# Weight loads on ScalarE's DMA queue, other transfers on the sync queue: a hybrid stick-breaking and retention step on one core

## The chip, the core and the metric

The kernel runs on one core of a Trainium2 chip. The metric is the device time of one execution in microseconds (us), as the median of several runs; lower is better. The core has five engines with a queue of instructions each: TensorE (PE, matrix products; its weight loads are listed as PEld), VectorE (DVE), ScalarE (ACT), GpSimd (POOL) and SyncE (SP). DMA transfers are issued by instructions that stand in the queue of SP, ACT or POOL; the profile writes such an entry as SPq or ACTq, and under POOL.

## The reference

One inference step of a one-layer encoder, all in float32. There are 1024 frames of a new prompt and 8 running streams of 16 frames (128 rows, "the sample"), each row 2048 wide.

```python
h = rms_norm(x, norm_pre)
q_sb, k_sb, v_sb, gate_sb, q_r, k_r, v_r, gate_r = split(h @ w_in)     # 8 x 1024 columns
q_r, k_r = rope(q_r, pos), rope(k_r, pos) * HEAD_DIM ** -0.5
# heads A (8 of 128): stick-breaking attention, strictly causal
a = exp(log_sigmoid(z) + reverse_cumsum_of(log_sigmoid(-z)));  o_sb = a @ v
# heads B (8 of 128): retention with a decay per head, in chunks of 64, with a running state S
o_r = (q k^T * decay) @ v + (q @ S) * decay_read;  S = S * g + k^T (v * decay_write)
y = concat(head_norm(o_sb) * silu(gate_sb), head_norm(o_r) * silu(gate_r)) @ w_out
x = x + rms_norm(y, norm_post)
```

The sample's attention also reads a cache of 1024 past keys and values per stream, its retention starts from a given state. Keys, values and states are outputs too.

## The kernel before

**Products.** Each float32 operand is split into a high part (ACT, a copy that rounds, line 166) and a low part (DVE, a subtraction, line 167), and each product is three matmuls: high by high, high by low, low by high. ACT and DVE therefore handle every block of weights before PE may use it. A raw block `wr` has five buffers, a split block `wh`/`wl` four.

**Stages.** The rows are worked in two groups. Group one (phase 0 in the code) holds row tiles 0 to 3 and the sample, 640 rows; group two (phase 1) holds tiles 4 to 7. Within a group the 8 heads follow each other. For a head, `rows_of_head` makes values and gates (`project_rows`, products at line 451, weights `wrn` loaded at line 442); `project` makes keys and queries of both kinds (products at line 394, weights `wr` loaded at line 383). Then follows the output product with `w_out` (lines 1195 to 1199, weights loaded at line 1212 by `load_split`), done with seven block products instead of eight, so that sums of operand blocks are made beforehand (`sums`, line 301) and left operands are loaded and split by `left` (lines 318 to 338).

**What runs beside the products.** Attention, retention, the head norms and the sums are generators ("jobs"). Each product calls `tick`, which advances a count and lets at most one due job do its next piece; the number that a job yields is the count of ticks until its next piece. The constants named `D_...` are these paces; of a pair, the first is for group one, the second for group two. From this the build fixes the order of the instructions in every engine's queue. A queue is then worked in that order, whatever is ready at run time.

**Rotary parts.** `rope` (line 491) reads a PSUM accumulator: ACT copies the swapped halves into `sw` (lines 495, 496), DVE multiplies `sw` by the sines (497), the accumulator by the cosines (498) and adds (499). The accumulator's bank is free for the next product when ACT's copies and the cosine product have read it. `sw` has one buffer.

**Turning tiles.** Several tiles are transposed by a way through DRAM: `turn_out` (line 634) writes the tile to a scratch tensor, `turn_in` (line 640) reads it back by four DMAs with exchanged block indices, and DVE transposes the 32x32 blocks. This is done for the retention keys (`s_rk`, lines 1016 to 1021), for each head's output (`s_o`, lines 703 to 717, in `Out.finish`), for the attention weights (`s_be`, by POOL) and for the sample's attention weights (`s_bd`).

**Row norms.** The root of each row's mean square is needed before values leave PSUM. `squares` (line 528) loads the rows and squares them on ACT: for group one during the first `rows_of_head`, for group two in a job started after it. `spread` (line 551) lays the roots out along a row by four matmuls (line 558).

**Queues.** SP issues the weight loads, the loads of rows, caches and operands and the read-backs `turn_in` of `s_rk`, `s_o` and `s_bd`. ACT issues the writes: `turn_out` of `s_rk`, `s_o`, `s_bd`, the stores of keys, values and states, of the sums, and the copy of the input rows into the output (`residuals`, line 367). POOL issues the loads of cached keys (line 802) and both ways of `s_be`.

Of the kernel before, what the change touches and what calls it, by code (L numbers as in the profile page):

```python
# [28 lines left out]
WQ = 4  # L29
D_X = (5, 4)  # L30
X_PIECES = ((0, 256), (256, 384), (640, 512))
# [15 lines left out]
D_TB = (17, 24)  # L47
D_TI = (36, 13)
D_OUT = 3
V_SET = 4  # L50
# [37 lines left out]
def tile_hybrid_step(  # L88
# [290 lines left out]
    def load_w(col):  # L379
        hs, ls = [], []  # L380
        for w in range(KT // WQ):
            wr = wp.tile([P, WQ, P], F32, name="wr", tag="wr", bufs=5)
            nc.sync.dma_start(wr, w_cols[COLS.index(col[0]), col[1], :, w * WQ : (w + 1) * WQ, :])
# [49 lines left out]
    def project_rows(g, mov, part, extra, out, loads=None, ready=None):  # L433
# [31 lines left out]
    with ExitStack() as s1:  # L465
# [25 lines left out]
        def rope(acc, tag, cosT, sinT):  # L491
            e = ep.tile([P, NMAX], F32, name=tag, tag=tag)
            for a, (o, m) in acc:
                sw = ep.tile([P, 512], F32, name="sw", tag="sw", bufs=1)
                nc.scalar.activation(sw[0:64, :m], a[64:128, :m], AF.Copy)
                nc.scalar.activation(sw[64:128, :m], a[0:64, :m], AF.Copy)
                nc.vector.tensor_tensor(sw[:, :m], sw[:, :m], sinT[:, o : o + m], ALU.mult)
                nc.vector.tensor_tensor(e[:, o : o + m], a[:, :m], cosT[:, o : o + m], ALU.mult)  # L498
                nc.vector.tensor_tensor(e[:, o : o + m], e[:, o : o + m], sw[:, :m], ALU.add)
            return e  # L500
# [11 lines left out]
        with tc.tile_pool(name="p0", bufs=2) as p0, tc.tile_pool(name="p0s", bufs=1) as p0s, tc.tile_pool(  # L512
# [48 lines left out]
            def second_panel(w):  # L561
                wr = wp.tile([P, WQ, P], F32, name="wr", tag="wr", bufs=5)
                nc.sync.dma_start(wr, w_cols[COLS.index(5), 0, :, w * WQ : (w + 1) * WQ, :])
# [51 lines left out]
            nc.scalar.dma_start(s_root, rb)  # L615

# [9 lines left out]
        def store_rows(tiles, n, dst_p, dst_s, h):  # L626
            nc.scalar.dma_start(dst_p[h, :, tiles[0] : tiles[0] + 4, :], n[:, :4, :])
            if SAMPLE in tiles:
                nc.scalar.dma_start(dst_s[h], n[:, 4, :])

        qp = kq.tile([P, 2, P], F32, name="qp")
        nc.vector.memset(qp, 0.0)

        def turn_out(src, tag, q=nc.scalar):

            s = scr.tile([src.shape[1], P, P], F32, name=tag)
            q.dma_start(s.rearrange("k q c -> q k c"), src)
            return s

        def turn_in(s, raw, q):  # L640
# [52 lines left out]
        class Out:  # L693
# [9 lines left out]
            def finish(self, b, gi, h, at, oT, dst):  # L703
# [12 lines left out]
                nc.vector.tensor_scalar(flat, oT[:, :n], gains[:, b, h : h + 1], None, ALU.mult)  # L716
                nc.scalar.dma_start(dst, flat)

# [176 lines left out]
        def retention(gi, g, h, out, rq, rk, rkn, rv, dT):  # L895
# [14 lines left out]
            for i in range(4):  # L910
# [31 lines left out]
                yield D_RET[phase[0]]  # L942
            nc.scalar.dma_start(s_S[h] if gi == 0 else s_prompt[0, 0, h], S)
            if SAMPLE in g["tiles"]:
                yield from sample_retention(h, out, sc, rq, rkn, rv)

        def sample_retention(h, out, sc, rq, rkn, rv):
# [57 lines left out]
            for c in range(4):  # L1005
                nc.scalar.dma_start(s_sample[h, :, 2 * c : 2 * c + 2, :], sts[c])

        def ret_branch(gi, g, h, rows_in, rk):
# [22 lines left out]
        def sb_branch(gi, g, h, out, q2, k2, kT, rest):  # L1031
            tiles, nt = g["tiles"], len(g["tiles"])
            off = 0 if gi == 0 else 4
            nc.scalar.dma_start(k_prompt[h, :, tiles[0] * P : (tiles[0] + 4) * P], kT[:, :NB_TOK])
            if SAMPLE in tiles:
                nc.scalar.dma_start(k_sample[h], kT[:, 4 * P : 5 * P])
            if gi == 0:
                nc.scalar.dma_start(s_k[h], kT[:, :NB_TOK])
            yield D_NAT[phase[0]]
            yield from stick_breaking(g, h, out, q2, k2, rest)  # L1040
            store_rows(tiles, values[gi, h][:, :, 0, :], v_prompt, v_sample, h)
            if gi == 0:
                nc.scalar.dma_start(s_v[h], values[gi, h][:, :4, 0, :])
            yield from out.finish(0, gi, h, 0, kT, s_y[gi][h][:, :NB_TOK])
# [238 lines left out]
    with ExitStack() as s3:  # L1283
# [78 lines left out]
        def all_of(made):  # L1362
# [60 lines left out]
        def keep_blocks():  # L1423
            for k in range(HT):
                wr = wp.tile([P, 512], F32, name="wr3", tag="wr", bufs=5)
                pin(nc.sync.dma_start(wr, weights_of(4, 1, k)))
                yield 1
# [143 lines left out]
```

## Time and profile before

| | us |
|---|---|
| median of 3 runs | 2281.82 (2278.89 to 2284.04) |
| the profiled execution's own time | 2282.22 |
| its span, first to last instruction | 2280.5 |
| PE busy in it | 2229.1 |
| DVE, ACT, POOL busy | 1272.2, 926.8, 343.7 |

The profile is one execution. Its page gives busy times, the chain of work that ended last and the costliest groups of instructions; the trace behind it answers narrower questions: who waited for whom, what ran in a given stretch, and when each DMA was issued. A row of the timeline has the start, the duration, engine, line, operation, the tiles written and read, the shape, a count where equal neighbours are merged, and in brackets the idle time of the engine before it with what ended it. A row of the waits has the waiting instruction, what it waited for, the total in us, the number of times and the longest. A row of the stretches has the stretch, its length, the busy time of PE, PEld, DVE, ACT and POOL (with counts), then the granted share of PE's clock, the DMA share and GB/s.

### The profile page before, as it was taken

The page shows a single profiled execution, that of the slowest core. Times are in us where ns is not written, and L with a number is a line of the kernel's source. Part 1 is how long each engine was busy: PE and PEld are TensorE (multiplying, and loading weights), DVE is VectorE, ACT ScalarE, POOL GpSimd, SP SyncE. Part 2 cuts the span into 40 slices and gives each one's busy share as a digit, 9 for nine tenths or more (in the row PEclk, how much of TensorE's full clock was granted, in tenths as well). Part 3 has the DMA queues.
Part 4 walks back from the last instruction along what each step waited for, and adds up shares of the span by engine and source line. Part 5 has one row for each costly group of instructions (what it writes and reads, how often), then busy time and mean ns, then how long its engine had stood idle before and what let it go on. Part 6 is the DMA issues. An engine that isn't in the chain of part 4 may idle for free.

```text
span 2280.5 us, 34787 instructions
## 1 busy us (share of the span) xinstructions
PE 2229.1 (98%) x12002; PEld 1891.4 (83%) x12002; DVE 1272.2 (56%) x2724; ACT 926.8 (41%) x1995; POOL 343.7 (15%) x577
## 2 busy tenths in 40 slices
PE   8999999999999999999999999999999999989998
PEld 7888889798888979797778888888888887768886
DVE  5345445453454445355556665656666657556667
ACT  6433333333333333334333343443433445545563
POOL 0011020212102020111202111120302113000020
PEclk9999999999999999999999999999999999999999
DMA  8566665576756657677768887888887777765785
GB/s 285 170 202 176 198 184 179 179 193 209 185 182 183 200 176 193 187 202 256 193 177 221 247 226 235 226 240 226 239 248 225 220 209 202 223 203 158 216 221 171
DMA packets 442354, 471.25 MB, mean 207 GB/s; under 512 B 182848, under 2 KB 298560, under 8 KB 441664
## 3 DMA queue, kind: packets, MB, share of 16 engines
q1 hardware_dynamic: 319936, 308.55, 46.7%
q0 software_dynamic: 28720, 78.41, 12.6%
q10 hardware_dynamic: 93520, 82.07, 11.4%
q8 instruction: 94, 1.54, 0.3%
q14 instruction: 84, 0.69, 0.1%
HBM read 367.97 MB, written 110.36 MB: 210 GB/s over the span
## 4 chain that ended last, share of the span: by engine, by line
PE 83%; DMA 6%; issue 4%; DVE 4%; ACT 2%; SPq 1%; ACTq 0%; DVEq 0%; POOL 0%; POOLq 0%
PE accm L451 34%; PE acc L394 27%; PE a L1195 4%; PE a L1199 4%; PE a L1198 4%; PE pa L777 2%; PE z L750 2%; PE zc L817 1%; PE pd L878 1%; DMA wr<-w_out 1%; DMA ro<-s_rk 1%; DMA mr<-s_s 1%; PE pa L917 1%; PE rs L899 1%; ACT wh L166 1%
## 5 line engine op out<-in xcount | busy, mean ns | idle before, releaser
L451 PE MATMUL accm<-whn,mh 128*128 128x512 f32 x1152 | 453.5, 394 | 4.0 <-DVE rq L498 3.9
L394 PE MATMUL acc<-mh,wh 128*128 128x256 f32 (+2 forms) x1536 | 445.0, 340 | 12.6 <-ACT wh L166 9.3
L451 PE MATMUL accm<-wln,mh 128*128 128x512 f32 x1152 | 452.5, 393 | 0.5 <-DVE wln L167 0.5
L451 PE MATMUL accm<-whn,ml 128*128 128x512 f32 x1152 | 452.9, 393 | 0.0
L394 PE MATMUL acc<-mh,wl 128*128 128x256 f32 (+2 forms) x1536 | 447.3, 342 | 0.3 <-DVE wl L167 0.3
L394 PE MATMUL acc<-ml,wh 128*128 128x256 f32 (+2 forms) x1536 | 446.4, 341 | 0.0
L166 ACT ACTIVATE wh<-wr 128x512 fp32r<-128x512 f32 x408 | 256.2, 631 | 466.3 <-PE acc L394 168.2
L167 DVE TENSOR_TENSOR wl<-wr,wh 128x512 fp32r<-128x512 f32 x408 | 278.8, 687 | 274.1 <-ACT wh L166 259.9
L167 DVE TENSOR_TENSOR wln<-wrn,whn 128x512 fp32r<-128x512 f32 x256 | 175.5, 689 | 290.4 <-ACT whn L166 279.2
L166 ACT ACTIVATE whn<-wrn 128x512 fp32r<-128x512 f32 x256 | 160.9, 632 | 413.3 <-PE accm L451 240.0
L394 PEld LDWEIGHTS acc<-mh,wh 128*128 128x128 f32 x1536 | 285.3, 190 | 31.9 <-ACT wh L166 9.5
L394 PEld LDWEIGHTS acc<-mh,wl 128*128 128x128 f32 x1536 | 283.2, 189 | 26.5 <-issue 6.8
L394 PEld LDWEIGHTS acc<-ml,wh 128*128 128x128 f32 x1536 | 282.7, 190 | 20.3 <-issue 1.2
L451 PEld LDWEIGHTS accm<-whn,mh 128*128 128x128 f32 x1152 | 217.0, 188 | 49.3 <-issue 2.6
L451 PEld LDWEIGHTS accm<-wln,mh 128*128 128x128 f32 x1152 | 217.0, 188 | 44.2 <-DVE wln L167 1.4
L451 PEld LDWEIGHTS accm<-whn,ml 128*128 128x128 f32 x1152 | 217.0, 188 | 43.8 <-issue 0.8
L802 POOL DMA_DIRECT2D kcT<-cache_k x64 | 34.8, 546 | 588.3 <-PE acc L394 404.9
L644 POOL DMA_DIRECT2D be<-s_be x128 | 94.0, 740 | 149.2 <-DMA s_be<-be 122.3
L680 DVE TENSOR_TENSOR_SCAN kp<-kp 128x1152 f32<-128x1152 f32 (+4 forms) x40 | 82.7, 2068 | 50.2 <-POOL kp L675 26.8
L1195 PE MATMUL a<-wh,mh 128*128 128x512 f32 x240 | 94.3, 395 | 6.1 <-ACT wh L166 3.7
L1199 PE MATMUL a<-wh,ml 128*128 128x512 f32 x240 | 94.3, 393 | 0.0
L1198 PE MATMUL a<-wl,mh 128*128 128x512 f32 x240 | 94.0, 392 | 0.0
(265 smaller groups left out, 2901.9 us busy)
## 6 DMA issues: line engine op xcount, KB each, us to landing
wr<-w_cols SPq DMA_DIRECT2D x256, 256.0 KB, 4.4
wrn<-w_rows SPq DMA_DIRECT2D x256, 256.0 KB, 3.9
kcT<-cache_k POOLq DMA_DIRECT2D x64, 512.0 KB, 4.9
vc<-cache_v SPq DMA_DIRECT2D x64, 512.0 KB, 5.3
wr<-s_b SPq DMA_DIRECT2D x80, 256.0 KB, 3.9
wr<-w_out SPq DMA_DIRECT2D x80, 256.0 KB, 3.8
br<-w_out SPq DMA_DIRECT2D x64, 256.0 KB, 4.1
s_b<-br ACTq DMA_DIRECT2D x32, 512.0 KB, 5.0
```

Source lines behind the costliest of these rows:

```text
L166: nc.scalar.activation(hi, src, AF.Copy),
L167: nc.vector.tensor_tensor(lo, src, hi.bitcast(F32), ALU.subtract),
L394: last = nc.tensor.matmul(a[:, :m], lhs[:, j, :], rhs[w][:, j, o : o + m], start=(w == 0 and j == 0 and n == 0), stop=(w == KT // WQ - 1 a ...
L451: anchor[0] = nc.tensor.matmul(banks[t], lhs[q][:, j, ts], rhs, start=(k == 0 and n == 0), stop=(k == KT - 1 and n == 2),)
L644: q.dma_start(raw[32 * i : 32 * i + 32, :].rearrange("p (k a) -> p k a", a=32), s[:, :, 32 * i : 32 * i + 32].rearrange("k (j b) a -> b (k ...
L680: nc.vector.tensor_tensor_scan(rev, rev, rev, 1.0, ALU.mult, ALU.bypass)
L750: nc.tensor.matmul(z[:, :c], q2[a][:, i * P : (i + 1) * P], k2[b][:, s : s + c], start=(m == 0), stop=(m == 2),)
L777: nc.tensor.matmul(po[:, :P], at[:, j, :], rest["vn"][j], start=(j == 0), stop=(j == t))
L802: ld = nc.gpsimd.dma_start(kc, cache_k[h, m // 4, m % 4])
L1195: ins = nc.tensor.matmul(a, hi[k][:, ts], wh, start=first, stop=False)
L1198: nc.tensor.matmul(a, hi[k][:, ts], wl, start=False, stop=False)
L1199: anchor[0] = nc.tensor.matmul(a, lo[k][:, ts], wh, start=False, stop=last)
```

## The change

- Every load of weights is issued by ACT's queue instead of SP's: lines 383, 442, 563, 1212 and 1426.
- What ACT's queue issued before, and the writes of `turn_out` by default, is issued by SP's queue: lines 314, 371, 615, 627, 629, 634, 717, 943, 1006, 1034, 1036, 1038 and 1043.
- The read-backs of `s_o` and `s_rk` are issued by POOL's queue in group one, and as before by SP's in group two. Those of `s_bd` stay with SP.
- In `rope` the product with the cosines stands ahead of the one with the sines.
- The squares of group two's rows are a job that begins when those of group one are done, inside the first `rows_of_head`, at a pace of 10 ticks instead of 4.
- Retention keys of group two are transposed 18 ticks after their read-back was issued instead of 13 (`D_RK`).
- The left operands of output block 2 are begun for group one of the rows in product (1, 0) and for group two in (1, 1), instead of both in (1, 1).

```diff
-D_X = (5, 4)
+D_X = (5, 10)
+D_RK = (36, 18)
...
-            pin(nc.scalar.dma_start(dst, r))
+            pin(nc.sync.dma_start(dst, r))
...
-                preset[t, c] = nc.scalar.dma_start(y_rows(t)[:, cs], x_rows(t)[:, cs])
+                preset[t, c] = nc.sync.dma_start(y_rows(t)[:, cs], x_rows(t)[:, cs])
...
-            nc.sync.dma_start(wr, w_cols[COLS.index(col[0]), col[1], :, w * WQ : (w + 1) * WQ, :])
+            nc.scalar.dma_start(wr, w_cols[COLS.index(col[0]), col[1], :, w * WQ : (w + 1) * WQ, :])
...
-            nc.sync.dma_start(wr, part[:, k, :])
+            nc.scalar.dma_start(wr, part[:, k, :])
...
+                nc.vector.tensor_tensor(e[:, o : o + m], a[:, :m], cosT[:, o : o + m], ALU.mult)
                 nc.vector.tensor_tensor(sw[:, :m], sw[:, :m], sinT[:, o : o + m], ALU.mult)
-                nc.vector.tensor_tensor(e[:, o : o + m], a[:, :m], cosT[:, o : o + m], ALU.mult)
...
             job = Job(squares(tiles, ssq[0], D_X[0]))
+
+            def after_first():
+                while not job.done:
+                    yield 2
+                yield from squares(GROUPS[1]["tiles"], ssq[1], D_X[1])
+
+            second = Job(after_first())
...
             rooted_tables((*first, *ropes), X_PIECES[:2])
-            job = Job(squares(GROUPS[1]["tiles"], ssq[1], D_X[1]))
-            tick()
             first.append(project(g0, mov, col(0, 0)))
-            drain(job)
+            drain(second)
...
-        def turn_out(src, tag, q=nc.scalar):
+        def turn_out(src, tag, q=nc.sync):
...
+        back = nc.gpsimd, nc.sync
...
-                turn_in(s, flat, nc.sync)
+                turn_in(s, flat, back[phase[0]])
...
-                nc.scalar.dma_start(dst, flat)
+                nc.sync.dma_start(dst, flat)
...
-            turn_in(s, raw, nc.sync)
-            yield D_TI[phase[0]]
+            turn_in(s, raw, back[phase[0]])
+            yield D_RK[phase[0]]
...
-            nc.sync.dma_start(wr, weights_of(n, nh, k))
+            nc.scalar.dma_start(wr, weights_of(n, nh, k))
...
-            (1, 1): ((2, BOTH),), (2, 1): ((5, G1),), (5, 0): ((3, G1),), (3, 0): ((6, BOTH),),
+            (1, 0): ((2, G0),), (1, 1): ((2, G1),), (2, 1): ((5, G1),), (5, 0): ((3, G1),), (3, 0): ((6, BOTH),),
```

The remaining lines of the diff exchange `nc.scalar` and `nc.sync` in the same way at the lines listed above.

More of the change, by code (lines that the diff above doesn't have):

```diff
@@ L562, in second_panel @@
                 wr = wp.tile([P, WQ, P], F32, name="wr", tag="wr", bufs=5)
-                nc.sync.dma_start(wr, w_cols[COLS.index(5), 0, :, w * WQ : (w + 1) * WQ, :])
+                nc.scalar.dma_start(wr, w_cols[COLS.index(5), 0, :, w * WQ : (w + 1) * WQ, :])
                 wh, wl = (p0s.tile([P, WQ, P], F32R, name=f"w{s}5{w}") for s in "hl")
@@ L614, in tile_hybrid_step @@
             spread(rb, root_of, len(tiles), last)
-            nc.scalar.dma_start(s_root, rb)
+            nc.sync.dma_start(s_root, rb)
         kq = s1.enter_context(tc.tile_pool(name="kq", bufs=1))
@@ L626, in store_rows @@
         def store_rows(tiles, n, dst_p, dst_s, h):
-            nc.scalar.dma_start(dst_p[h, :, tiles[0] : tiles[0] + 4, :], n[:, :4, :])
+            nc.sync.dma_start(dst_p[h, :, tiles[0] : tiles[0] + 4, :], n[:, :4, :])
             if SAMPLE in tiles:
-                nc.scalar.dma_start(dst_s[h], n[:, 4, :])
+                nc.sync.dma_start(dst_s[h], n[:, 4, :])
         qp = kq.tile([P, 2, P], F32, name="qp")
         nc.vector.memset(qp, 0.0)
-        def turn_out(src, tag, q=nc.scalar):
+        def turn_out(src, tag, q=nc.sync):
             s = scr.tile([src.shape[1], P, P], F32, name=tag)
@@ L942, in retention @@
                 yield D_RET[phase[0]]
-            nc.scalar.dma_start(s_S[h] if gi == 0 else s_prompt[0, 0, h], S)
+            nc.sync.dma_start(s_S[h] if gi == 0 else s_prompt[0, 0, h], S)
             if SAMPLE in g["tiles"]:
@@ L1005, in sample_retention @@
             for c in range(4):
-                nc.scalar.dma_start(s_sample[h, :, 2 * c : 2 * c + 2, :], sts[c])
+                nc.sync.dma_start(s_sample[h, :, 2 * c : 2 * c + 2, :], sts[c])
         def ret_branch(gi, g, h, rows_in, rk):
@@ L1033, in sb_branch @@
             off = 0 if gi == 0 else 4
-            nc.scalar.dma_start(k_prompt[h, :, tiles[0] * P : (tiles[0] + 4) * P], kT[:, :NB_TOK])
+            nc.sync.dma_start(k_prompt[h, :, tiles[0] * P : (tiles[0] + 4) * P], kT[:, :NB_TOK])
             if SAMPLE in tiles:
-                nc.scalar.dma_start(k_sample[h], kT[:, 4 * P : 5 * P])
+                nc.sync.dma_start(k_sample[h], kT[:, 4 * P : 5 * P])
             if gi == 0:
-                nc.scalar.dma_start(s_k[h], kT[:, :NB_TOK])
+                nc.sync.dma_start(s_k[h], kT[:, :NB_TOK])
             yield D_NAT[phase[0]]
@@ L1042, in sb_branch @@
             if gi == 0:
-                nc.scalar.dma_start(s_v[h], values[gi, h][:, :4, 0, :])
+                nc.sync.dma_start(s_v[h], values[gi, h][:, :4, 0, :])
             yield from out.finish(0, gi, h, 0, kT, s_y[gi][h][:, :NB_TOK])
@@ L1425, in keep_blocks @@
                 wr = wp.tile([P, 512], F32, name="wr3", tag="wr", bufs=5)
-                pin(nc.sync.dma_start(wr, weights_of(4, 1, k)))
+                pin(nc.scalar.dma_start(wr, weights_of(4, 1, k)))
                 yield 1
```

## The prediction

> **What bounds the kernel now.** I read the page first, for the share of PE.
>
> ```profile
> span 2280.5 us, 34787 instructions
> ...
> PE 2229.1 (98%) x12002; PEld 1891.4 (83%) x12002; DVE 1272.2 (56%) x2724; ACT 926.8 (41%) x1995; POOL 343.7 (15%) x577
> ```
>
> PE is busy all but 2280.5 - 2229.1 = 51.4 us. The change takes no matmul away, so it can only win from those 51 us and from time in which PE runs at a lower clock. Where they lie comes from the stretches; the two long ones are nearly all of both groups.
>
> ```profile
> 118.25:1046.00 927.75, 923.91 (x5786) 805.01 (x5786) 442.48 (x1017) 320.32 (x698) 156.11 (x287) 1.00 0.66 192
> 1153.00:1889.00 736.00, 731.67 (x3527) 612.44 (x3526) 467.01 (x939) 299.32 (x637) 129.98 (x201) 1.00 0.79 227
> ```
>
> In these 1664 us PE idles 3.8 and 4.3 us, and its clock is full. There is almost nothing to win in the body of either group, and much to spoil. The loss sits at the start, at the change of groups (1046 to 1153) and where the output product begins (1889 on). PE's waits tell who ended each idle time.
>
> ```profile
> PE acc L394 <- ACT wh L166: 9.3, 2, 7.1
> PE a L1195 <- ACT wh L166: 5.5, 3, 3.7
> PE accm L451 <- DVE rq L498: 3.9, 2, 2.1
> PE acc L394 <- DVE rk L498: 3.4, 1, 3.4
> PE pSs L996 <- DVE st L1000: 2.6, 1, 2.6
> PE pb L558 <- DVE dg L556: 2.6, 1, 2.6
> PE a L1195 <- ACT ml L1255: 2.5, 1, 2.5
> PE pS L932 <- DVE rkn L1025: 2.3, 2, 1.2
> ```
>
> These eight rows hold 32 us, 7.1 of it the start. Most waits come once: single places, not a rate. Last I asked for the stretches in which the clock is granted at half.
>
> ```profile
> 114.84:118.25 3.41, 3.04 (x13) 3.01 (x14) 1.36 (x9) 0.60 (x2) 0.00 (x0) 0.50 0.62 190
> 1050.10:1056.90 6.80, 5.40 (x14) 4.36 (x15) 3.93 (x8) 4.42 (x7) 0.00 (x0) 0.50 0.87 277
> 1121.80:1128.60 6.80, 6.63 (x30) 5.38 (x34) 4.68 (x14) 2.18 (x6) 0.00 (x0) 0.50 0.24 80
> 1145.70:1152.40 6.70, 5.82 (x14) 4.60 (x15) 3.76 (x9) 1.81 (x3) 0.00 (x0) 0.50 0.68 161
> 2026.40:2033.10 6.70, 4.76 (x11) 3.79 (x12) 3.81 (x7) 3.98 (x8) 0.00 (x0) 0.50 0.76 255
> ```
>
> Each follows one of the waits above. PE does in them half of what it would do, so they cost half of its busy time: 1.5, 2.7, 3.3, 2.9 and 2.4 us. A gap of 2.6 us thus costs about 4 to 6 us.
>
> The Trainium skill, "TensorE: Matmul & The Clock Gate", section on HAM oscillation, gives the rule that PE-idle gaps should not exceed about 3.4 us. By it the gaps of 2.6 us (L558, L996) and of 2.1 us (L451) would have cost no clock, and the sum below would lose 2.9 us of its gain. The rows show half clock behind all three, so the sum goes by the rows.
>
> **The change, part by part.** Against the profiled execution's 2282.2 us.
>
> *Squares of group two sooner.* PE waits for the roots of group two at the end of the first query product.
>
> ```profile
> 50.00:118.00 68.00, 65.41 (x333) 57.23 (x332) 22.89 (x62) 32.44 (x61) 0.00 (x0) 0.98 0.57 189
> ```
> ```profile
> 109.47 1.06 ACT L542 ACTIVATE xt<-xt 128x1024 f32<-128x1024 f32 x1
> ```
> ```profile
> 115.21 1.22 PE L558 MATMUL pb<-dg,ones 128*128 128x128 f32 x4 [2.59 <-DVE dg L556]
> ```
>
> The last square ends at 110.53, and 4.7 us later the first `dg` lets PE go on. By the code, ten squares of group one at 5 ticks end about tick 55 of the first `rows_of_head`, which has 16 x 5 x 3 x 0.75 = 180; eight more at 10 ticks end about tick 145. So they are done before PE begins the query product. ACT, busy 32.4 of 68 us here with the squares counted, covers them; without that cover they would delay splits by 1.1 us each. Gone: 2.6 + 1.5 = 4.1 us.
>
> *Cosines first.* At the change of groups PE waits twice for a bank.
>
> ```profile
> 1046.02 0.38 ACT L496 ACTIVATE sw<-acc 64x256 f32<-64x256 f32 x1
> ```
> ```profile
> 1047.85 0.42 DVE L498 TENSOR_TENSOR rq<-acc,cosT 128x256 f32<-128x256 f32 x1
> ...
> 1050.81 0.55 DVE L498 TENSOR_TENSOR rq<-acc,cosT 128x384 f32<-128x384 f32 x1
> ```
>
> The first bank could be free when ACT has copied, at 1046.40, not at 1048.27: the first wait, 3.9 - 2.1 = 1.8 us, goes. For the second bank the cosines move ahead of one product of the same size, 0.55 us, and next late are ACT's copies. That is 2.4 us; half the clock loss of 2.7 is taken as gone with it. Total 3.7 us; bounds 0.6 (only one product's length) and 6.6.
>
> *Outputs of group one: store by SP, read-back by POOL.* The wait of 3.4 us for `rk` L498 is no matter of the cosines, because that product writes `rk`, and `finish` of the head before still uses `rk` as its transposed output.
>
> ```profile
> 1120.17 0.58 DVE L740 STREAM_TRANSPOSE kb<-kb 128x384 f32<-128x384 f32 x1 [5.10 <-DMA kb<-s_be]
> ...
> 1129.10 1.40 DVE L706 SCALAR_TENSOR_TENSOR ro<-ro,or,gg 128x128 f32<-128x128 f32 x5
> ...
> 1145.15 0.55 DVE L716 TENSOR_SCALAR ro<-rk,gains 128x640 f32<-128x640 f32 x1
> 1145.74 0.69 DVE L498 TENSOR_TENSOR rk<-acc,cosT 128x512 f32<-128x512 f32 x1
> ```
> ```profile
> 1132.06 0.38 ACTq L637 DMA_DIRECT2D s_o<-ro  x1
> ```
> ```profile
> 1138.35 2.07 SPq L644 DMA_DIRECT2D ro<-s_o  x4
> ```
>
> The tile is ready at 1130.50, ACT stores it at 1132.06, SP reads it back from 1138.35. On SP the store gains up to 1.6 us, and on POOL the read-back no longer stands behind weights; the 6.3 us between the two include that queue. If the chain is 3.4 us quicker in all, the wait is gone with its clock loss: 6.3 us. I take 5.0; bounds 0 and 6.3. POOL's own later work, masks and the read-back of `s_be`, now stands behind these. That read-back keeps DVE waiting 5.10 us at 1120, which ends in PE's 2.6 us at L996 plus 3.3 of clock. I take 0 there, with bounds of a gain of 5.9 and a loss of 3.
>
> *Weights on ACT's queue.* At two places weights come late because SP stands at something else.
>
> ```profile
> 229.91 3.11 SPq L644 DMA_DIRECT2D so<-s_o  x4
> 233.12 8.06 SPq L383 DMA_DIRECT2D wr<-w_cols  x7
> ```
> ```profile
> 238.26 2.19 ACT L166 ACTIVATE wh<-wr 128x512 fp32r<-128x512 f32 x4 [3.08 <-DVE do L706]
> ```
> ```profile
> 2027.66 0.63 ACT L166 ACTIVATE wh<-wr 128x512 fp32r<-128x512 f32 x1 [0.22 <-DMA wr<-w_out]
> ```
>
> At 233 SP issues seven loads in a row behind read-backs, and ACT's four splits at 238 come behind a store that waited on DVE; the store leaves ACT. The wait of 2.2 us (9.3 - 7.1) goes; I take 2.0. From 2005 three waits for `wh`, 5.5 us, and 2.4 of clock have late `w_out` blocks behind them. Loads of left operands stay on SP and no longer hold weights up, and part of the left splits is moved a product earlier. I take 6.0 of 7.9, bounds 0 and 7.9. The 2.5 us for `ml` L1255 is an eviction behind other ACT work: 0.5. With the later transposition of group two's keys, 1.5 of the 2.3 us for `rkn` go.
>
> Gains: 4.1 + 3.7 + 5.0 + 2.0 + 6.0 + 0.5 + 1.5 = 22.8 us.
>
> *What ACT pays.* Every load waits until DVE has read the buffer that it fills.
>
> ```profile
> L167 DVE TENSOR_TENSOR wl<-wr,wh 128x512 fp32r<-128x512 f32 x408 | 278.8, 687 | 274.1 <-ACT wh L166 259.9
> L167 DVE TENSOR_TENSOR wln<-wrn,whn 128x512 fp32r<-128x512 f32 x256 | 175.5, 689 | 290.4 <-ACT whn L166 279.2
> ```
>
> 408 + 256 = 664 loads. An issue on ACT takes 0.38 us by the row at 1132.06, so 252 us; if each also waits one whole low split, 0.69, another 458 us. ACT would be held 927 + 710 = 1637 of 2280 us at worst, without counting the stores that leave. It does not become the bound. Behind a waiting load stand ACT's evictions and sigmoids, for which PE and DVE wait; split weights have four buffers of cover. None of this is in the trace. The low end is 0, the high end the rival below; I take a quarter of 0.38 + 0.69 in each of 16 heads, 4 us, nearer to 0 because ACT is idle more than half of the time. The start stays at 7.1, since ACT's first split waits for data that is issued no sooner than now.
>
> Sum: 2282.2 - 22.8 + 4 = 2263.4, so **2263 us**; the profiled execution is 0.4 us above the median, which changes nothing.
>
> **Rivals.** *Only the edits of order pay.* The split blocks lie up to four ahead, so a late load may be caught up anyway, and what ended the late waits was other work of ACT. Then squares, cosines and the later key turn remain: 4.1 + 3.7 + 1.5 = 9.3, so 2273. For it speaks that weights caused only 7.7 us of waits without the start; against it the rows at 229 and 233. The Trainium skill, "DMA: Bandwidth & Descriptors", section "Issuing engines are not separate DMA queues", says that issuing from several engines saves only the sequencer's issue time. By that rule this rival would hold; the row at 229.91 shows SP held by read-backs ahead of weights, a wait in the queue that the rule does not count.
>
> *Slower: ACT's queue passes DVE's stalls on.* DVE waits for read-backs, as the 5.10 us at 1120 show. A load then holds ACT, whose evictions come late, and PE stops inside the bodies that now idle 8 us in 1664. At 0.38 + 0.69 = 1.07 us an event, three events in each of 16 heads cost 51 us: 2282 - 23 + 51 = 2310; two events, 34 us, give 2293. It decides from 22 late events on. Against it stands that ACT waits for PE, not the reverse, in almost all of the body.
>
> *No change.* The order in the queues comes out so that read-backs on POOL and stores on SP wait as long as before and the late blocks stay late; or the first events of the slower rival eat the gain. About 2280.
>
> **How the numbers follow.** Forecast (2250 to 2269) 0.55; only order, 2273, 0.16; no change 0.11; slower, 2288 to 2310, 0.18. A measurement of this kernel can tell about 0.2%, 4.6 us, from no change. So faster 0.71, same 0.11, slower 0.18. The range starts at 2248, where nearly every bound is taken at its best (4.1 + 6.6 + 6.3 + 5.9 + 7.9 + 2.0 + 1.5 = 34 and no cost), and ends at 2291, short of two late events in each head, which leaves out about 2 in 10.
>
> **What would show it.** Right: no wait at L558 and none for `rk` at the change of groups; fewer half-clock stretches than five; no late `wh` after 2005; both bodies still idle under 10 us together. Wrong: PE waits inside the bodies for tiles that ACT evicts, or DVE's waits for POOL's read-backs grow; or the gaps after 2005 are as they were.

## The result and the profile after

The changed kernel takes 2314.39 us (median of 5 runs, 2306.93 to 2318.77) against 2281.82 us (5 runs, 2278.89 to 2285.2). The ratio is 1.0149, 95% interval 1.013 to 1.0168: slower by some 33 us, where 2263 us was forecast, and outside the range. The profiled execution is the one of 2314.39 us. First its page:

```profile
span 2312.5 us, 34591 instructions
...
PE 2238.9 (97%) x12002; PEld 1891.6 (82%) x12002; DVE 1276.5 (55%) x2724; ACT 927.2 (40%) x1993; POOL 417.8 (18%) x705
```

PE is now idle for 2312.5 - 2238.9 = 73.6 us instead of 51.4, and busy 9.8 us longer with the same 12002 matmuls. ACT's busy time, in which DMA issues are not counted, has not changed. Its 672 loads of weights, at 0.33 to 0.41 us an issue in the rows below, would add some 240 us (an estimate), so ACT as a whole did not become the bound. PE's waits say where to look:

```profile
PE acc L395 <- ACT mh L172: 23.7, 2, 23.2
PE a L1203 <- ACT wh L167: 9.3, 12, 2.8
...
PE a L1206 <- DVE wl L168: 4.8, 10, 1.3
PE accm L452 <- DVE rq L498: 4.0, 2, 2.5
...
PE acc L395 <- DVE rk L498: 3.7, 1, 3.7
PE a L1203 <- ACT mh L1263: 3.6, 1, 3.6
PE pSs L1004 <- DVE st L1008: 1.5, 1, 1.5
```

The start has grown from 7.1 to 23.2 us, the output product (L1203, L1206) waits 22 times for late blocks of weights, the two waits of the change of groups (`rq` and `rk` L498) are as long as before, and the wait for the roots (L558) is gone.

For the bookkeeping, each product of PE is compared with the same product in the other traces: the 9600 matmuls on `acc`, `accm` and `a` come in nearly the same order in all kernels, and the table gives how much later (or sooner, negative) the product stands than in the kernel before. A column minus the one ahead of it is what the stretch between lost.

| product that began before at (us) | 7.1 | 125.4 | 257.9 | 1016.2 | 1180.4 | 1823.1 | 2043.4 | 2269.9 |
|---|---|---|---|---|---|---|---|---|
| changed kernel | +16.1 | +12.6 | +9.8 | +9.5 | +11.3 | +9.4 | +20.7 | +32.5 |
| start's weights on SP | +0.2 | -5.2 | -8.0 | -8.2 | -7.6 | -7.7 | +6.5 | +15.5 |
| output product's weights on SP | +15.8 | +12.1 | +9.3 | +9.0 | +9.5 | +10.8 | +14.5 | +14.5 |
| both | 0.0 | -5.3 | -8.1 | -8.4 | -7.4 | -9.6 | -0.4 | -0.4 |
| before, writes on SP | -0.1 | -0.2 | +3.0 | +3.1 | +3.0 | +7.7 | +8.5 | +8.5 |
| both, group two's writes on ACT | +0.5 | -4.3 | -7.1 | -7.4 | -5.1 | +12.2 | +9.7 | +9.7 |
| and group two's weights on SP | +0.2 | -4.4 | -7.2 | -7.5 | -2.8 | -3.3 | -4.1 | -4.1 |
| and the last head's pace at 6 | -0.3 | -5.9 | -8.7 | -9.0 | -10.7 | -8.9 | -12.0 | -12.0 |
| before, squares and pace alone | -0.7 | -1.7 | -0.2 | -0.2 | -4.4 | -4.2 | -5.9 | -5.9 |

Each row is one execution. With 1.9 us around the span, as in the changed kernel, they lie within 3 us of the medians given below, but for three: the run with the output product's weights on SP was traced 4 us under its median, the one with the writes alone on SP 3.5 under, and the one with group two's writes on ACT 7 over; their stretches are read with that much doubt.

So the changed kernel loses 16.1 us at the start, wins some 6 up to 258 us, holds level through both groups, and loses 23.1 us from 1823 on. Where do the 16 us come from? The timeline of the changed kernel's start, ACT and then SP:

```profile
0.81 0.41 ACTq L384 DMA_DIRECT2D wr<-w_cols  x1
...
4.59 0.63 ACT L167 ACTIVATE wh<-wr 128x512 fp32r<-128x512 f32 x1 [1.85 <-DMA wr<-w_cols]
4.60 0.35 ACTq L384 DMA_DIRECT2D wr<-w_cols  x1
...
11.54 0.63 ACT L167 ACTIVATE wh<-wr 128x512 fp32r<-128x512 f32 x1 [4.11 <-DMA wr<-w_cols]
...
22.12 0.63 ACT L167 ACTIVATE wh<-wr 128x512 fp32r<-128x512 f32 x1 [6.75 <-DMA wr<-w_cols]
22.66 0.89 ACT L172 ACTIVATE mh<-xc,pre 128x256 fp32r<-128x256 f32 x2
```
```profile
1.25 13.53 SPq L526 DMA_DIRECT2D xc<-x_cols  x8
```

ACT issues the first load at 0.81, but the third only at 4.60, behind a split that waited for the first one. Six splits of weights stand in ACT's queue ahead of the first split of `xc` (`mh` L172), although SP had issued all of `xc` by 14.8. In the kernel before the first split of `xc` comes as soon as that block has landed, and the two kinds alternate behind it:

```profile
5.66 0.91 ACT L171 ACTIVATE mh<-xc,pre 128x256 fp32r<-128x256 f32 x2 [3.35 <-DMA xc<-x_cols]
```

In the changed kernel the blocks also take 8.0 us to land, in its list of transfers up to 40 us, beside the eight loads of `xc` (5.6 up to 24 us in the kernel before); the second experiment parts the two causes:

```profile
wr<-w_cols ACTq DMA_DIRECT2D x8, 256.0 KB, 8.0
```

Of the six stretches of half clock the first two, and the sum of all six:

```profile
1058.37:1065.19 6.82, 5.07 (x12) 3.68 (x13) 5.16 (x12) 5.46 (x9) 0.00 (x0) 0.50 0.81 282
1130.05:1136.87 6.82, 6.77 (x30) 4.99 (x34) 4.05 (x12) 1.90 (x4) 0.00 (x0) 0.50 0.54 114
...
sum 34.11, PE 29.89 PEld 23.28 DVE 21.43 ACT 13.66 POOL 7.40; mean PE 4.98 PEld 3.88 DVE 3.57 ACT 2.28 POOL 1.23
```

There were five; the one after the squares (115 us) and the one at 2026 us are gone, and three are new in the overlap of the last heads with the output product (from 1911.70, 1949.25 and 1962.90). That they cost half of PE's busy time in them, 29.9 / 2 = 15 us against 12.8 in the five of before, explains 2 of PE's 9.8 us of longer busy time. Part of the rest is waiting that the rows hide. Matmuls of this size are listed at 0.39 us but start 0.23 us apart, so the first 0.16 us of a wait counts as busy:

```profile
2270.74 0.39 PE L1207 MATMUL a<-wh,ml 128*128 128x512 f32 x1
2270.97 0.39 PE L1206 MATMUL a<-wl,mh 128*128 128x512 f32 x1
```

The end of the output product shows it without any half clock. From the product at 2043.4 to the last one, in the kernel before and then in the changed kernel:

```profile
2043.42:2269.86 226.44, 226.44 (x1001) 187.50 (x999) 149.04 (x308) 116.81 (x262) 19.82 (x23) 1.00 0.66 188
```
```profile
2064.12:2302.40 238.28, 229.94 (x1001) 186.71 (x999) 149.83 (x308) 118.32 (x262) 19.75 (x23) 1.00 0.64 177
```

PE never waited there before. Now 22 matmuls start late, and the stretch is 11.8 us longer: 8.3 of them show as idle, 3.5 as longer busy time.

The late blocks at the end, in the timeline of ACT and one row of PE:

```profile
2246.95 0.63 ACT L167 ACTIVATE wh<-wr 128x512 fp32r<-128x512 f32 x1 [1.67 <-DMA wr<-s_b]
...
2247.83 1.23 ACTq L1220 DMA_DIRECT2D wr<-s_b  x2
2254.38 1.30 ACT L167 ACTIVATE wh<-wr 128x512 fp32r<-128x512 f32 x2 [5.93 <-DMA wr<-s_b]
```
```profile
2275.29 0.73 PE L1203 MATMUL a<-wh,mh 128*128 128x512 f32 x2 [2.80 <-ACT wh L167]
```

It is the pattern of the start: two loads, a wait for them, two splits, and only then the next load. On ACT's queue the loads have lost their lead over the splits.

### The profile page after: what moved, and what is told of

It is laid out like the page before. It is cut to its first block, busy times and chain, and to the rows that moved or that the text cites. A ratio compares the mean times of both kernels' runs of the same rounds, so it can differ in the third digit from the quotient of the medians.

```text
span 2312.5 us, 34591 instructions
## 1 busy us (share of the span) xinstructions
PE 2238.9 (97%) x12002; PEld 1891.6 (82%) x12002; DVE 1276.5 (55%) x2724; ACT 927.2 (40%) x1993; POOL 417.8 (18%) x705
## 3 DMA queue, kind: packets, MB, share of 16 engines
q10 hardware_dynamic: 96768, 176.20, 25.6%
## 5 line engine op out<-in xcount | busy, mean ns | idle before, releaser
L395 PEld LDWEIGHTS acc<-ml,wh 128*128 128x128 f32 x1536 | 282.6, 190 | 20.7 <-issue 2.1
L1203 PE MATMUL a<-wh,mh 128*128 128x512 f32 x240 | 95.5, 401 | 8.2 <-ACT wh L167 4.6
L1206 PE MATMUL a<-wl,mh 128*128 128x512 f32 x240 | 95.6, 399 | 1.9 <-DVE wl L168 1.9
```

The costliest lines, as they stand in the source:

```text
L395: last = nc.tensor.matmul(a[:, :m], lhs[:, j, :], rhs[w][:, j, o : o + m], start=(w == 0 and j == 0 and n == 0), stop=(w == KT // WQ - 1 a ...
L1203: ins = nc.tensor.matmul(a, hi[k][:, ts], wh, start=first, stop=False)
L1206: nc.tensor.matmul(a, hi[k][:, ts], wl, start=False, stop=False)
```

## The experiments

The theory: an ACT queue that holds both the loads and the splits of weights turns loading ahead into round trips, at the start (16 us) and in the output product (the greater part of 23 us). The rivals: the transfers themselves became slower (at the start 8.0 us instead of 5.6, but in the output product the median landing of `wr<-s_b` is 3.7 us, 3.9 before); or the writes on SP, or the left operands begun a product sooner, make the loss.

**The start's weights on SP.**

```diff
-            first_panel = load_w(col(4, 0))
+            first_panel = load_w(col(4, 0), nc.sync)
...
-                nc.scalar.dma_start(wr, w_cols[COLS.index(5), 0, :, w * WQ : (w + 1) * WQ, :])
+                nc.sync.dma_start(wr, w_cols[COLS.index(5), 0, :, w * WQ : (w + 1) * WQ, :])
```

> The changed kernel with only the sixteen weight blocks of the start (lines 384 for the first panel, and 564) issued by SP again, so that they alternate with the loads of xc as before. Queue theory: of the 32 us lost, 16 are the start, where ACT's queue holds six splits of weights ahead of the first split of xc; with the old order PE's first matmul is at 7 to 8 us instead of 23.2 and the time is 2314 - 16 = 2298 us, ratio to before 1.007. Rival (the start is only shifted: what PE does later is bound by other things, such as late loads at the end): the start comes back but less than 8 us of the time does, 2306 or more.

2296.44 us, ratio to before 1.0075 (1.0051 to 1.0098). PE begins as early as before (table, +0.2). 18 us come back; the shift of the start was a loss in full, and the rival falls.

**Loads of `xc` on ACT too.** It keeps the start's weights on ACT but lets them alternate with `xc` again.

```diff
-                nc.sync.dma_start(xc, src[:, k : k + m, :])
+                nc.scalar.dma_start(xc, src[:, k : k + m, :])
```

> The changed kernel with the loads of xc issued by ACT as well, so that loads of weights and of xc alternate again as they did on SP, while all eight splits of weights now stand ahead of the first split of xc in ACT's queue. Queue theory (ACT waits in order for eight blocks before it begins xc): PE still starts late, at 13 to 20 us, since some 4 MB must land at about 350 GB/s ahead of the eighth split. Rival (the weights only landed late, 8.0 us each, because eight loads of xc were issued at once on SP): with the loads alternating the first matmul is at 7 to 9 us and the time falls by 14 us or more.

One run, 2314.01 us. PE begins at 25.6 us, later still, although the blocks land in 4.3 us instead of 8.0. PE's first product, the list of transfers, and ACT's timeline, which shows why:

```profile
25.63 0.80 PE L395 MATMUL acc<-mh,wh 128*128 128x256 f32 x2 [25.63 <-ACT mh L172]
```

```profile
wr<-w_cols ACTq DMA_DIRECT2D x8, 256.0 KB, 4.3
```
```profile
14.53 0.33 ACTq L384 DMA_DIRECT2D wr<-w_cols  x1
...
18.29 1.30 ACT L167 ACTIVATE wh<-wr 128x512 fp32r<-128x512 f32 x2 [3.14 <-DMA wr<-w_cols]
...
23.02 1.33 ACT L167 ACTIVATE wh<-wr 128x512 fp32r<-128x512 f32 x2 [3.43 <-DMA wr<-w_cols]
...
25.07 1.31 ACT L172 ACTIVATE mh<-xc,pre 128x256 fp32r<-128x256 f32 x3 [0.72 <-issue]
```

Each round trip of two loads, landing and two splits takes 4.5 to 5 us, and all eight splits stand ahead of `xc`. Crowded transfers are not the cause; the order in the queue is. It came in later than the 13 to 20 us expected, because the estimate counted bytes, not round trips.

**The output product's weights on SP.** Start as in the changed kernel.

```diff
-            nc.scalar.dma_start(wr, weights_of(n, nh, k))
+            nc.sync.dma_start(wr, weights_of(n, nh, k))
...
-                pin(nc.scalar.dma_start(wr, weights_of(4, 1, k)))
+                pin(nc.sync.dma_start(wr, weights_of(4, 1, k)))
```

> The changed kernel with only the weight loads of the output product (lines 1220 and 1434) issued by SP again; start and input projections as in the changed kernel. Queue theory (an in-order ACT queue issues the blocks of the output product too late, behind its own splits, evictions and scalings): of the 23 us lost from 1823 on, 15 to 21 come back, 2293 to 2299 us, ratio 1.005 to 1.008; the waits on wr<-s_b (19 us in 13 waits of ACT) fall to about the 2.3 us of before. Rival (stores on SP ahead of the loads of left operands, or the left split moved into product (1, 0), make the loss): less than 6 us come back, 2308 or more, with the waits of ACT for mr<-s_y (17 us) still there.

2300.33 us, ratio 1.0088 (1.0063 to 1.0114): 14 us come back, 1 less than the theory's least. After 2043 us nothing is lost any more (table). ACT's waits in the output product, in the kernel before and in the changed kernel:

```profile
ACT wh L166 <- DMA wr<-s_b: 2.3, 3, 1.0
```
```profile
ACT wh L167 <- DMA wr<-s_b: 19.0, 13, 5.9
...
ACT mh L167 <- DMA mr<-s_y: 17.4, 9, 3.2
```

and in this run:

```profile
ACT mh L167 <- DMA mr<-s_y: 5.9, 6, 1.5
...
ACT wh L167 <- DMA wr<-s_b: 1.5, 1, 1.5
```

The waits for `wr<-s_b` are back at the length of before, as expected, and those for `mr<-s_y` are shorter too, against the rival.

**Both.** The two edits together.

> Both of the above: ACT issues only the weights of the input projections behind the start. Queue theory: the two losses are at different places and add, so 2314 - 16 - 18 = 2280, ratio 0.997 to 1.001; with the squares (-4.2), the place at 236 (-2.8) and group two's keys (-1.9) kept, the start at 7 to 8 us and 1.8 us lost at the change of groups, it could reach 2275, ratio 0.997. Rival (the losses overlap, or other edits carry the output product's loss): 2290 or more.

2282.64 us, ratio 1.0007 (0.9994 to 1.002). The losses add: 18 and 14 us, the same in each order of taking them back. But it ties with before although it stands 9.6 us ahead at 1823 us: 9.2 us go between 1823 and 2043. That stretch in the kernel before, then in this run:

```profile
1823.07:2043.42 220.35, 207.87 (x958) 169.85 (x956) 137.82 (x275) 112.11 (x235) 28.58 (x44) 0.98 0.75 214
```
```profile
1813.46:2043.03 229.57, 215.05 (x957) 172.33 (x956) 140.36 (x277) 112.41 (x237) 29.94 (x44) 0.97 0.74 208
```

No single wait holds it: idle time is 14.5 us against 12.5, and PE is busy 7.2 us longer, with half clock for 13.7 us against 6.8 and with hidden waiting as above.

**Squares alone,** on the kernel before (`D_X = (5, 10)` and the new job of the diff).

> The kernel before with only the squares of group two begun inside the first block of rows (pace 10). Theory (places add up; what is won early stays won): no wait for the roots of group two, PE 4.2 us earlier from 120 us on and also at the end, 2281 - 4.2 = 2277 us, ratio 0.998. Rival (the stretch from 1823 to 2043 is bound by a chain beside PE, which gives back what was won ahead of it; the run with weights of start and output on SP stood 9.6 us ahead at 1823 and 0.4 us ahead at the end): PE is 4.2 us ahead at 1823 and less than 1 us ahead at the end, 2281 us, ratio 1.000.

2276.45 us, ratio 0.9989 (0.9978 to 0.9999), 2.5 us won. The interval, a gain of 0.2 to 5.0 us, holds the 4.2 expected and leaves out the rival's ratio of 1.000, if only just. In the trace, of an execution 3.8 us above the median, the step at the place itself is 4.1 us; the first block of rows, beside which the squares now run, lost 1.7 ahead of it. PE is 1.7 us ahead at 258 us, 0.5 at 1823 and 1.9 at the end. So nothing won early was given back from 1823 on, though with 0.5 us to give back the trace is a weak test of the rival.

**Writes alone on SP,** on the kernel before.

```diff
-            pin(nc.scalar.dma_start(dst, r))
+            pin(nc.sync.dma_start(dst, r))
...
-        def turn_out(src, tag, q=nc.scalar):
+        def turn_out(src, tag, q=nc.sync):
```

> The kernel before with only the writes that ACT issued (keys, values, states, sums, outputs, the ways out of turned tiles, the copy of the input) issued by SP; all weights stay on SP. Theory (the 9 us lost in the overlap of the last heads with the output product come from writes that stand among SP's loads: a write waits for DVE, and the loads behind it wait too): 5 to 9 us are lost from 1823 to 2043 and up to 3 us at the place of the sample's outputs near 236 us, 2286 to 2293 us, ratio 1.002 to 1.005. Rival (the loss comes from the other edits in that stretch, the left split begun earlier or the later key turn): within 3 us of before, ratio 0.999 to 1.001.

2293.73 us, ratio 1.0065 (1.0046 to 1.0085), 14 us lost, more than the theory's 1.005. The table has 3.2 us at 236, as expected, and 4.7 in group two, which were not; in the same bookkeeping it is 15.4 us at 1937, and 7 of these are made up until 2043. Writes between SP's loads are costly. But from 1823 to 2043, where the theory had placed 5 to 9 us, the net loss is 0.8: the place was missed, and writes on SP alone don't make the overlap's 9 us. In the run with both edits, where the projections' weights had left SP, the place at 236 and the body of group two lost nothing (table), but the overlap did.

**Cosines alone,** on the kernel before.

```diff
-                nc.vector.tensor_tensor(sw[:, :m], sw[:, :m], sinT[:, o : o + m], ALU.mult)
                 nc.vector.tensor_tensor(e[:, o : o + m], a[:, :m], cosT[:, o : o + m], ALU.mult)
+                nc.vector.tensor_tensor(sw[:, :m], sw[:, :m], sinT[:, o : o + m], ALU.mult)
```

> The kernel before with only the cosine product ahead of the sine product in the rotary part. Theory (the cosine product of a bank does not begin before ACT has copied that bank, in either order, so only the place of one product in DVE's queue changes): the two waits at the change of groups for the bank fall by at most 0.6 us each, with no change of the clock's loss; 2279 to 2282 us, ratio 0.999 to 1.000. Rival, the prediction's step: both waits shrink by 1.8 us, 3.7 us in all with the clock, 2278 us, ratio 0.998, and none of it is lost again.

2278.2 us, ratio 1.0 (0.9983 to 1.0016): no gain to be seen. The interval alone reaches to a gain of 3.9 us and would just leave room for the prediction's 3.7, but the two waits are as long as before (3.9):

```profile
PE accm L451 <- DVE rq L497: 4.0, 2, 2.8
```

The reason is in two rows of the changed kernel:

```profile
1060.64 0.48 ACT L497 ACTIVATE sw<-acc 64x384 f32<-64x384 f32 x1
```
```profile
1061.15 0.56 DVE L498 TENSOR_TENSOR rq<-acc,cosT 128x384 f32<-128x384 f32 x1 [1.13 <-ACT sw L497]
```

The cosine product does not read `sw`, yet DVE idles 1.13 us until ACT's copy of the same bank is done. ACT's copies are written ahead of it, and the second reader of the bank follows the first; whether the two DVE products are exchanged changes nothing in that.

**The left operands of block 2 as before,** on top of both.

> The changed kernel with the weights of start and output product on SP (2282.6 us), and the left operands of output block 2 begun for both groups in product (1, 1) as before. Theory (the loss from 1823 to 2043 is made by the writes on SP): the loss stays, 2280 to 2284 us. Rival (the left split in product (1, 0) takes ACT and SP at the stage where the last heads still run): the waits from 1988 to 2043 (3.1 us more than before) go, 2277 to 2280 us.

2279.89 us, ratio 1.0002 (0.999 to 1.0014), on the edge between the two expectations. The trace decides: PE is still 9.2 us ahead at 1823 and 1.3 at the end, and PE's waits for `wh` L1203 from 1975 us on are 7.5 us against 5.3 in the run with both. Beginning them sooner is not the cause.

**Group two's writes on ACT again,** on top of both.

```diff
+    def writes():
+        return (nc.sync, nc.scalar)[phase[0]]
...
-            pin(nc.sync.dma_start(dst, r))
+            pin(writes().dma_start(dst, r))
...
```

> As the run with start and output weights on SP, and the writes of group two and of the output product (also the sums and the copy of the input) issued by ACT again; writes of group one stay on SP, weights of the projections stay on ACT in both groups. Theory (writes among SP's loads make the 9 us lost from 1823 to 2043): PE is still 9 us ahead of before at 1823 and at least 6 us at the end, 2271 to 2275 us, ratio 0.996 to 0.998. Rival (late blocks of the output product take the gain back whoever issues the writes, since that stretch ends by data that come at a time of their own): 2279 to 2282 us, ratio 0.999 to 1.001.

2284.19 us, ratio 1.0018 (1.0008 to 1.0027): a miss, slower. The overlap loses nothing more (from +12.2 to +9.7), but the body of group two loses 17.3 us in the traced execution, which is 7 us over the median. PE's waits between 1165 and 1830 us:

```profile
PE rs L913 <- DVE rq L506: 6.3, 3, 2.2
```

One of them in the timeline of DVE and of PE:

```profile
1248.85 0.71 DVE L1035 STREAM_TRANSPOSE rkn<-ro 128x512 f32<-128x512 f32 x1 [1.65 <-DMA ro<-s_rk]
1249.49 0.65 DVE L506 TENSOR_TENSOR rq<-rq,sw 128x512 f32<-128x512 f32 x1
```
```profile
1250.19 0.71 PE L913 MATMUL rs<-rq,rk 128*128 128x128 f32 x4 [1.90 <-DVE rq L506]
```

DVE stands at a read-back that has not landed, with the rotary sum behind it and PE behind that. This is the slower rival of the prediction in its own place, the bodies, though through DVE's queue rather than ACT's evictions. In the changed kernel itself it does not occur.

**Group two's weights on SP as well.**

```diff
+    def weights_by():
+        return (nc.scalar, nc.sync)[phase[0]]
...
-            nc.scalar.dma_start(wr, part[:, k, :])
+            weights_by().dma_start(wr, part[:, k, :])
```

> As the run before this one in this list, with the weights of group two's projections issued by SP as well, so that from group two on the queues are those of the kernel before. Theory: the same 2271 to 2275 us, since weights on ACT cost nothing in the bodies (the body of group one moved by 0.0 us). Rival (the weights on ACT hold ACT where the last heads overlap the output product): 3 us or more faster than the run before this one.

2277.63 us, ratio 0.9994 (0.9981 to 1.0006). 6.6 us faster than the run before: the rival's expectation, though in the body and not in the overlap. Of both losses, the overlap's (9.2) and the body's (17.3), nothing is left after 1180 (table: -2.8 to -4.1). It stays short of 2271 to 2275 because the change of groups cost 4.6 us here, with one wait of 5.8 us:

```profile
PE rs L914 <- DVE rq L507: 7.4, 5, 5.8
```

**The last head of group one sooner,** on top of that.

```diff
+        def pace_of(h):
+            return 6 if (phase[0], h) == (0, H - 1) else D_RET[phase[0]]
...
-            yield D_RET[phase[0]]
+            yield pace_of(h)
```

> As the run before this one in this list, with the retention of group one's last head at a pace of 6 ticks instead of 9, so that its last steps are put sooner into the engines' queues. Theory (at the change of groups PE waits for the turned output because of its place in DVE's queue, behind two splits of weights, and not because of the way through DRAM): the wait for rk L498 of 3.7 us falls under 1.5 us and one stretch of half clock goes, 3 to 6 us faster than the run before this one, 2266 to 2271 us. Rival (the way through DRAM, store 4.7 us and read-back 2.7 and 3.8 us, sets the end): the wait stays over 3 us, since DVE then waits for the data.

2269.7 us, ratio 0.9949 (0.9936 to 0.9962), the fastest of all, 7.9 us under the run before and 10 us under the runs of before beside it (2279.82). That is more than the 3 to 6 us expected: the wait of 5.8 us that the run before had at the change of groups is gone as well. The wait for `rk` is gone from the list and so is `pSs`. In the changed kernel DVE turned the output 1.5 us ahead of the rotary product; here, in the second fence, 4.7 us ahead. Both fences are rows of DVE:

```profile
1153.04 0.84 DVE L723 STREAM_TRANSPOSE rk<-ro 128x640 f32<-128x640 f32 x1
...
1154.50 0.69 DVE L498 TENSOR_TENSOR rk<-acc,cosT 128x512 f32<-128x512 f32 x1
```
```profile
1116.52 0.84 DVE L730 STREAM_TRANSPOSE rk<-ro 128x640 f32<-128x640 f32 x1
...
1121.17 0.69 DVE L505 TENSOR_TENSOR rk<-acc,cosT 128x512 f32<-128x512 f32 x1 [0.53 <-ACT sw L504]
```

This does not part the theory from its rival, since the pace moves the way through DRAM sooner too: the tile is stored at 1094.4 instead of 1122.5. The changed kernel's own trace says more. There the last read-back has landed at 1151.3, and DVE turns the tile at 1153.0: at most 1.7 of the 3.7 us of the wait are its place in DVE's queue, and the rest is not told apart.

The other wait of that place grew from 3.9 us:

```profile
PE accm L459 <- DVE rq L505: 7.8, 2, 5.1
```

**Squares and pace alone,** no queue moved.

> The kernel before with two edits of pace and none of queues: the squares of group two begun sooner, and the retention of group one's last head at 6 ticks instead of 9. Theory (what paid in the fastest run so far, 2269.7 us, is the places of steps in the engines' queues, not the queues of the DMAs): the waits for rk L498 (3.4 us) and pSs (2.6 us) at the change of groups go with two stretches of half clock, as they did there, 2268 to 2273 us, ratio 0.995 to 0.997. Rival (the store by SP and the read-back by POOL were needed for it as well): the wait for rk stays over 2 us, 2275 us or more, ratio 0.998.

2274.94 us, ratio 0.9973 (0.9963 to 0.9984). The waits for `rk` and `pSs` are gone without SP's stores and POOL's read-backs, so these were not needed for it. In the table the change of groups (1016 to 1180) wins 4.2 us, where squares alone won 0.1 in their trace. The time, 2274.9, lies between the two expectations. At the end it stands 6.1 us behind the run ahead of it (-5.9 and -12.0), and the table has all of that by 258 us (-0.2 and -8.7): the queues of group one pay there, for the squares and at the place near 236 us.

## Why the prediction was wrong, point by point

- *"The start stays at 7.1, since ACT's first split waits for data that is issued no sooner than now."* This step failed most dearly: 16.1 us at PE's first product, 17.6 by the one that began at 13.2, 18 in the runs. It looked at when the data is issued and not at what stands in ACT's queue: loads behind splits, and the splits of weights ahead of those of `xc`. The build made that order anew when the loads changed engine. A diff does not show it, so the start should have had a bound above zero.
- *Weights after 2005: gain 6.0, bounds 0 and 7.9.* The sign was wrong: 14 us lost by the output product's weights, shown twice (2314.4 to 2300.3 and 2296.4 to 2282.6). The prediction saw that left operands no longer stood ahead of weights on SP, and missed that on ACT the same loads stand behind splits and behind waits for left operands. What those loads lose behind 2043 us alone is 11.8.
- *Writes on SP: no term.* The prediction counted the writes only as relief for ACT ("without counting the stores that leave") and put nothing for where they go. Alone they cost 14 us (ratio 1.0065); beside weights on ACT they are part of the 9 us of the overlap.
- *Squares: 4.1.* Right at the place (4.1 to 4.2 in every trace that has the edit), and L558 is off the list. Alone they are worth 2.5. There the first rows lost 1.7 beside them, so on the kernel before "ACT covers them" was too kind; in the changed kernel those rows lose nothing (16.8 us late from 50 to 105 us).
- *Cosines: 3.7, bounds 0.6 and 6.6.* Failed: the waits stay, 4.0 us, and the ratio is 1.0. The wait for ACT's copy holds in either order.
- *Outputs of group one: 5.0.* Failed: the wait is 3.7 us, 3.4 before. The store did go sooner, by SP at once, and POOL read back, but DVE turns the tile at its place in the queue, behind two splits, 1.7 us after it has landed. The last two runs show that steps put sooner into the queues end the wait, the last one without SP's store and POOL's read-back; how much of the wait is DVE's queue alone they don't show. *`kb`: 0*, within its bounds: `pSs` 1.5 instead of 2.6, with the same half clock behind it.
- *Weights at 239: 2.0.* Right, 2.8 in the trace. *`rkn`: 1.5.* Right as to the waits: both are gone. The body's 1.9 us are not firm: with the same edits it won 0.1 with the start's weights on SP and 2.2 with both, and lost 1.3 with the output product's. *`ml` L1255: 0.5.* Wrong, it became a wait of 3.6 us for `mh` L1263 in the same eviction.
- *What ACT pays: 4 us over 16 heads.* 0.0 in the body of group one, none to be seen in group two. The price was looked for where ACT has slack and not where it has none.
- *The rivals.* "Slower, 2288 to 2310" had the right sign but was placed in the bodies, at two or three events a head; there were none there, and 2314.4 is above it. A loss of that kind in a body, 17.3 us, appeared only when writes joined the weights on ACT; the writes alone on SP lost 4.7 in group two. What the prediction named as signs of being wrong, "the gaps after 2005 are as they were", was the nearest to what happened.

Not settled is what costs the overlap its 9 us. It shows with writes on SP and group two's weights on ACT together (9.2, and 7.9 with the left operands as before). With writes on SP and all weights there it is 0.8, with both kinds on ACT it is gone, and in the fastest run, which also comes to the overlap 9 us ahead, it is gone too. Nor is it a fixed price: with the same queues as "both" it was 3.7 us in the trace of the run with only the output product's weights on SP, where PE comes 20 us later to that stretch. How much of it is PE's coming early, which the runs that come late don't pay, is not told apart.

## What to carry to other kernels

A load belongs on a queue whose earlier entries don't wait for earlier loads: moved onto the engine that consumes the data, loading ahead becomes a round trip per pair, and the price shows first where there is no lead yet (the start) or the consumer is busiest (the end: ACT 49% busy from 1890 us on, 40% over all), not on average. Before moving DMA issues, write down for each queue what stands ahead of each load, not when its data would be free. A tile that is late at a fixed place may be late by its place in a queue: moving its producer's steps sooner (one pace, 4.2 us at the change of groups with no queue moved) paid where other queues for its transfers did not.

## What the runs showed of the hardware

*Read-backs land later beside another engine's loads.* The group two read-backs of the keys (64 KB each, always issued by SP, 1180 to 1850 us) in the kernel before, with the writes alone on SP, in the changed kernel, and last with writes and weights of group two on ACT:

```profile
ro<-s_rk SPq DMA_DIRECT2D x24, 64.0 KB, 3.6
```
```profile
ro<-s_rk SPq DMA_DIRECT2D x24, 64.0 KB, 3.7
```
```profile
ro<-s_rk SPq DMA_DIRECT2D x24, 64.0 KB, 6.7
```
```profile
ro<-s_rk SPq DMA_DIRECT2D x24, 64.0 KB, 7.5
```

With the weights on SP's queue the median is 3.6 and 3.7 us, and 4.8 in the run with group two's weights on SP as well; with the weights on ACT's it is 5.9 (both), 6.7 and 7.5. A read-back that lands late is what DVE waits for in the row at 1248.85. Why they land later is open. The Trainium skill, "DMA: Bandwidth & Descriptors", section "Issuing engines are not separate DMA queues", says that transfers of several engines interleave on the same DMA engines and that issuing from several saves only the small time of the issue. The first half doesn't explain these rows, since by it the transfers share the engines in all four kernels; the second leaves out the waits in the queue, 18 and 14 us here.

*Half clock does not go by the length of the gap alone.* The wait of 1.5 us for `pSs` (L1004) is followed by half clock, the stretch from 1130.05 above; the one of 2.80 us ahead of L1203 at 2275.29 is not:

```profile
2275.29:2282.00 6.71, 6.71 (x30) 5.55 (x30) 5.04 (x8) 3.44 (x8) 0.00 (x0) 1.00 0.03 10
```

The prediction priced each gap of over 2 us with half clock behind it; in the output product that was too dear, and near the change of groups a shorter one paid as well. What else decides, no run here shows.
